# Seven products for eight in six weight pairs of eight, half of their weight sums added by a DMA, and two small regroupings

## The chip, the cores and the metric

The kernel runs on one core of one Trainium2 chip. The metric is the device time of one execution in microseconds (us); lower is better. Engines are named as the profile names them: PE (TensorE: matmuls, with their weight loads shown apart as PEld), DVE (VectorE), ACT (ScalarE), POOL (GpSimd) and SP (SyncE, which here only issues DMAs).

## The reference, cut to what matters

Two layers over 256 rows of width 2048, all in float32. Each layer is a mixer and an MLP, each between two RMS norms:

```python
for l in range(DEPTH):
    g = norm_g[l]
    u = rmsnorm(h, g[0])
    ...                                    # mixer: input projection, two head groups, output projection
    h = h + rmsnorm(y, g[1])
    u = rmsnorm(h, g[2])
    z = jnp.square(jax.nn.relu(u @ mlp_w1[l])) @ mlp_w2[l]
    h = h + rmsnorm(z, g[3])
```

`mlp_w1[l]` is 2048 x 8192, `mlp_w2[l]` is 8192 x 2048. The change lies in `u @ mlp_w1[l]`, which the kernel calls the first half of the MLP ("up"), and at the seam between the output projection and the MLP.

## The kernel before, in words

**Tiles.** The 256 rows are two tiles (t = 0, 1) of 128. A product runs with a 128x128 piece of the activations as stationary operand and a 128x512 piece of the weights as moving operand, into a PSUM bank of 128x512. To keep float32 accuracy every operand is split in two float32r parts, hi = the rounded value and lo = the rest, and a product takes three matmuls: x_hi·w_hi, x_hi·w_lo, x_lo·w_hi.

**Weights.** SP loads a weight tile `raw` of two 128-row slabs by 512 columns (512 KB). ACT casts it to `whi` (L223, or L331 in the MLP's first half), DVE subtracts to get `wlo` (L224, L332). There are 7 buffers for `raw` and 6 pairs for `whi`/`wlo`; a pair comes free when PE has done the last product that reads it, and a cast waits for a free pair.

**The MLP.** Its 8192 hidden columns are taken in 8 chunks of 1024. `up(c)` computes a chunk, `down(c)` multiplies it with `mlp_w2`. The order in the code is up(0), up(1), down(0), up(2), down(1), ..., up(7), down(6), down(7). Chunk 0 runs with ordinary blocks (`Block`), chunks 1 to 7 with `Pairs`; both layers do this, so there are 14 `Pairs` blocks in all.

**Pairs.** A `Pairs` block has eight steps s. Step s takes two slabs of 128 weight rows, 1024 columns wide, in two raw tiles: L (the first 512 columns) and R (the last 512), each with rows 0 and 1. This is a 2 x 2 block product: (t = 0, 1) x (row 0, 1) times (row 0, 1) x (L, R). The string `PAIRS`, one letter a step, says how it is computed:
- "C", ordinary: 8 products, that is 24 matmuls, into four banks p2, bR, q4, q3, with L and R cast as they are.
- "S", summed: the Strassen-Winograd form with 7 products (21 matmuls), called p1, p2, q3, q5, p7, p6, q4 in this order, each with a PSUM bank of its own over all steps. It needs sums of the activation blocks (made once a layer by `Differences`, L294 to L305) and of the weights: R1+R0 and R0+L0, from which `two` is cast, then L0+(R1+R0) and L1+(that), from which `four` is cast.

Before, `PAIRS` is "CSCSSCSS". `Pairs.load(s)` for an S step does, in the order of the code: the cast of L (`plain`), the cast of R's row 1 (`r1`), two DVE additions in place on R (L336), the cast of R (`two`), two DVE additions in place on L (L336), the cast of L (`four`). So an S step takes four pairs of `whi`/`wlo`, a C step two.

At the last step, which is an S, the block's results are combined from the seven banks on DVE (L383, L397, L398), with p1 and bR copied out by ACT (L387, L372), and `evac` applies the squared ReLU (L598).

**Order on the engines.** Each engine, and each DMA queue, works its instructions in a fixed order that is set when the program is built. The builder may place an instruction ahead of one that stands earlier in the code; what waits on what is kept by semaphores.

**The seam.** `out_proj` ends with four weight steps that run first for t = 0 and then for t = 1 (TAIL). `between(t)` follows each: it finishes the norm of the projection (L551, L552), adds to h (L509), transposes h for the next products (`prenorm_x`: PE L175, ACT L166, DVE L168), sums the squares of h on ACT (`sumsq_of`, L489) for the second norm, and stores h by POOL's DMA (L532). up(0) starts with six weight steps (LEAD) run for t = 0 alone, then `lead_in` calls `between(1)`, then the same six run for t = 1. The factor of the second norm is not needed before the last chunk of the MLP, since a squared ReLU lets it be applied late.

Of the kernel before, what the change touches and what calls it, by code (L numbers as in the profile page):

```python
# [22 lines left out]
NT = 2  # L23
# [4 lines left out]
PAIRS = "CSCSSCSS"  # L28
# [11 lines left out]
def trunk(ctx, tc, x, x_t, norm_g, ng_cols, e_win, rbf, e_wout, o_win, lbraw, smalls, wa2, ba, o_wout, w1, w2,  # L40
# [269 lines left out]
    class Pairs:  # L310
# [13 lines left out]
        def load(self, s):  # L324
            raws = [rawp.tile([P, SLAB, 512], F32, name="raw") for _ in range(2)]
            for raw, n in zip(raws, (self.n0, self.n0 + 512)):
                nc.sync.dma_start(out=raw, in_=self.wv[:, 2 * s:2 * s + 2, n:n + 512])

            def conv(raw, i=slice(0, SLAB)):
                hi, lo = w_pair()  # L330
                nc.scalar.copy(out=hi[:, i, :], in_=raw[:, i, :])  # L331
                nc.vector.tensor_tensor(out=lo[:, i, :], in0=raw[:, i, :], in1=hi[:, i, :], op=ALU.subtract)  # L332
                return hi, lo

            def add(dst, a, b):
                nc.vector.tensor_tensor(out=dst, in0=a, in1=b, op=ALU.add)  # L336
# [12 lines left out]
            self.w[s] = [plain, r1, two, conv(L)]  # L349

        def product(self, n, s, x, w, i):
            first = n not in self.ps
            if first:
                self.ps[n] = accp.tile([P, 512], F32, name="acc") if n in ("bR", "p2", "p1") else aux()
            ps, (xh, xl), (hi, lo) = self.ps[n], x, w
            done = s == self.nslab - 1 or n == "bR" and "C" not in PAIRS[s + 1:]
            nc.tensor.matmul(ps, xh, hi[:, i, :], start=first, stop=False)  # L357
            nc.tensor.matmul(ps, xh, lo[:, i, :], start=False, stop=False)  # L358
            nc.tensor.matmul(ps, xl, hi[:, i, :], start=False, stop=done and not (n == "bR" and i == 0))  # L359

        def mm(self, s, t):
# [4 lines left out]
            z = self.ps  # L366
            if PAIRS[s] == "C":
# [9 lines left out]
            s1, u, u3, zb = self.U  # L377
            out = {}

            def comb(n, a, b, op):  # L380
                if n not in out:
                    out[n] = self.evac.tile()
                nc.vector.tensor_tensor(out=out[n], in0=a, in1=b, op=op)  # L383

# [4 lines left out]
            if end:  # L389
                comb("aL", z["p2"], s1, ALU.add)  # L390
                self.evac(0, 0, out["aL"])
# [8 lines left out]
            if end:  # L400
                comb("aR", z["q5"], u, ALU.subtract)
                comb("aR", z["q3"], out["aR"], ALU.add)
                self.evac(0, 1, out["aR"])
                comb("bL", z["q4"], u3, ALU.add)
                self.evac(1, 0, out["bL"])
                comb("bR", z["q5"], u3, ALU.subtract)
                comb("bR", zb, out["bR"], ALU.add)
                self.evac(1, 1, out["bR"])
# [128 lines left out]
    def out_proj(l, w, kts, X2, y, X, ypool, spool, src, mid):  # L537
# [25 lines left out]
        return rst, lambda: between(1)  # L563

    def mlp(l, X, rst, y, ypool, spool, mid, between, lead):
# [11 lines left out]
        def lead_in():  # L577
            lead()
            for t in range(NT):
                pre[t] = powers(rst[t])  # L580
# [48 lines left out]
        def scratch():  # L629
            for _ in range(2):  # L630
                u = spool.tile([P, 2, 512], F32, name="s")
                U.extend(u[:, i, :] for i in range(2))
# [78 lines left out]
    def feed_forward(l, w, kts, X2, src, between):  # L711
        pools = [tc.tile_pool(name=f"yp{l}", bufs=1), tc.tile_pool(name=f"sp{l}", bufs=7)]
# [3 lines left out]
        rst, lead = out_proj(l, w, kts, X2, y, X, yp, sp, src, mid)  # L716
        mlp(l, X, rst, y, yp, sp, mid, lambda t, r, h: between(t, r, h, y, yp), lead)()
# [495 lines left out]
```

## Time and profile before

| | |
|---|---|
| time, median of 3 runs | 2261.35 us (2261.01 to 2261.88) |
| the profiled execution's own time | 2261.99 us |
| its span, first to last instruction | 2260.2 us |
| mean granted TensorE clock | 0.999 |
| PE busy | 2238.3 us, 99% of the span |
| DVE busy | 1750.7 us, 77% |
| ACT busy | 1173.7 us, 52% |
| DMA queue of SP (q1) | 429.18 MB, 59.1% of 16 engines' span |
| DMA queue of POOL (q0) | 8.99 MB, 1.1% |

A row of instructions reads: line of the kernel, engine, operation, output tile <- input tiles, shapes, count | busy us, mean ns of one | idle time of the engine before them and what ended it. A row of a timeline reads: start in us from the start of the span, duration in us, engine, line, operation. A matmul's duration is that of one matmul in a pipeline: the next one starts before it ends, so PE's pace is read from start to start.

### The profile page before, as it was taken

Reading aid. Unit: us, or ns where it says so; the run is one execution under the profiler, and the core shown is the slowest. Engines: PE = TensorE matmul, PEld = TensorE weight load, DVE = VectorE, ACT = ScalarE, POOL = GpSimd, SP = SyncE. Lnnn points to the kernel's source line nnn. Section 1 sums busy time; section 2 is a strip of 40 time slices with the busy share of each in tenths; the row PEclk is TensorE's granted clock in tenths of the full one; section 3 lists DMA queues with packets and bytes.
Section 4 is the critical chain, followed back from the end, with each engine's and each line's share of the span. In section 5 each row is a group of like instructions: output and inputs, shape, how many; then the busy total and the mean of one; then the engine's idle time right before and its main releaser. Section 6 shows DMA issues by size and latency. Waiting matters only on the chain.

```text
span 2260.2 us, 28830 instructions
## 1 busy us (share of the span) xinstructions
PE 2238.3 (99%) x10556; PEld 1850.9 (82%) x10556; DVE 1750.7 (77%) x2328; ACT 1173.7 (52%) x1612; POOL 20.7 (1%) x40
## 2 busy tenths in 40 slices
PE   9999999999999999999999999999999999999998
PEld 7888887888888888888788888887888888888886
DVE  6656656988898898896867767657979789789786
ACT  7444445655454454454746454546555445445453
POOL 0000000000000000000100000000000000000000
PEclk9999999999999999999999999999999999999999
DMA  9565576565665665676655555576565565665673
GB/s 344 168 182 168 168 268 186 181 222 165 198 216 160 211 198 184 205 242 221 213 172 166 153 151 153 173 237 194 169 205 195 187 206 184 197 205 177 214 263 102
DMA packets 222559, 440.87 MB, mean 195 GB/s; under 512 B 13744, under 2 KB 14544, under 8 KB 222416
## 3 DMA queue, kind: packets, MB, share of 16 engines
q1 hardware_dynamic: 218880, 429.18, 59.1%
q0 software_dynamic: 2816, 8.99, 1.1%
q8 instruction: 83, 1.36, 0.3%
q10 hardware_dynamic: 720, 0.85, 0.1%
q14 instruction: 60, 0.49, 0.1%
HBM read 430.57 MB, written 8.40 MB: 194 GB/s over the span
## 4 chain that ended last, share of the span: by engine, by line
PE 75%; DVE 14%; issue 5%; ACT 4%; DMA 1%; ACTq 0%; DVEq 0%; SPq 0%
PE acc L237 18%; PE acc L238 17%; PE acc L236 17%; DVE raw L336 4%; DVE wlo L332 4%; PE acc L275 3%; PE aux L275 3%; ACT whi L331 3%; DVE wlo L224 2%; PE aux L272 2%; PE acc L272 2%; DVE ulo L383 2%; PE aux L359 2%; PE aux L357 2%; PE aux L358 2%
## 5 line engine op out<-in xcount | busy, mean ns | idle before, releaser
L224 DVE TENSOR_TENSOR wlo<-raw,whi 128x1024 fp32r<-128x1024 f32 (+1 forms) x561 | 676.2, 1219 | 303.9 <-ACT whi L223 301.9
L223 ACT CAST whi<-raw 128x1024 fp32r<-128x1024 f32 (+1 forms) x561 | 582.5, 1053 | 587.1 <-PE acc L238 464.7
L331 ACT CAST whi<-raw 128x1024 fp32r<-128x1024 f32 x364 | 343.5, 969 | 372.3 <-DVE raw L336 213.8
L237 PE MATMUL acc<-wlo,x 128*128 128x512 f32 x1280 | 502.7, 393 | 1.9 <-DVE wlo L224 0.6
L238 PE MATMUL acc<-whi,x 128*128 128x512 f32 x1280 | 498.8, 390 | 0.0
L236 PE MATMUL acc<-whi,x 128*128 128x512 f32 x1280 | 497.1, 392 | 0.0
L332 DVE TENSOR_TENSOR wlo<-raw,whi 128x1024 fp32r<-128x1024 f32 x364 | 397.9, 1119 | 106.2 <-ACT whi L331 99.4
L237 PEld LDWEIGHTS acc<-wlo,x 128*128 128x128 f32 x1280 | 240.3, 188 | 59.2 <-DVE wlo L224 10.8
L236 PEld LDWEIGHTS acc<-whi,x 128*128 128x128 f32 x1280 | 240.3, 188 | 50.6
L238 PEld LDWEIGHTS acc<-whi,x 128*128 128x128 f32 x1280 | 240.4, 188 | 49.1
L236 PE MATMUL acc<-whi,xt 128*128 128x512 f32 x640 | 254.1, 399 | 0.5 <-ACT xt L671 0.5
L237 PE MATMUL acc<-wlo,xt 128*128 128x512 f32 x640 | 251.6, 394 | 3.0 <-DVE wlo L224 3.0
L238 PE MATMUL acc<-whi,xt 128*128 128x512 f32 x640 | 250.8, 392 | 0.0
L336 DVE TENSOR_TENSOR raw<-raw 128x512 f32<-128x512 f32 x280 | 193.8, 692 | 9.3
L237 PEld LDWEIGHTS acc<-wlo,xt 128*128 128x128 f32 x640 | 120.8, 189 | 29.6 <-DVE wlo L224 6.2
L236 PEld LDWEIGHTS acc<-whi,xt 128*128 128x128 f32 x640 | 120.6, 189 | 25.7 <-ACT xt L671 1.4
L238 PEld LDWEIGHTS acc<-whi,xt 128*128 128x128 f32 x640 | 120.5, 188 | 25.3 <-issue 0.3
L357 PE MATMUL acc<-whi,xt 128*128 128x512 f32 x308 | 120.0, 390 | 0.0
L359 PE MATMUL acc<-whi,xt 128*128 128x512 f32 x308 | 119.8, 389 | 0.0
L358 PE MATMUL acc<-wlo,xt 128*128 128x512 f32 x308 | 119.8, 389 | 0.0
L358 PE MATMUL aux<-wlo,s 128*128 128x512 f32 x280 | 110.6, 395 | 1.9 <-DVE wlo L332 0.2
L357 PE MATMUL aux<-whi,s 128*128 128x512 f32 x280 | 109.2, 390 | 0.0
(230 smaller groups left out, 2551.2 us busy)
## 6 DMA issues: line engine op xcount, KB each, us to landing
raw<-w SPq DMA_DIRECT2D x512, 512.0 KB, 4.5
raw<-o_win SPq DMA_DIRECT2D x112, 512.0 KB, 3.8
raw<-e_win SPq DMA_DIRECT2D x95, 512.0 KB, 3.9
raw<-e_wout SPq DMA_DIRECT2D x32, 512.0 KB, 4.2
raw<-o_wout SPq DMA_DIRECT2D x32, 512.0 KB, 3.7
s<-norm_g SPq DMA_DIRECT2D x8, 512.0 KB, 4.6
mid<-s POOLq DMA_DIRECT2D x8, 512.0 KB, 3.5
s<-mid SPq DMA_DIRECT2D x8, 512.0 KB, 5.7
```

Source lines behind the costliest of these rows:

```text
L223: nc.scalar.copy(out=hi[:, a:b, n], in_=raw[:, a:b, n])
L224: nc.vector.tensor_tensor(out=lo[:, a:b, n], in0=raw[:, a:b, n], in1=hi[:, a:b, n], op=ALU.subtract)
L236: nc.tensor.matmul(ps, xh, hi[:, i, 0:self.n], start=first, stop=False)
L237: nc.tensor.matmul(ps, xh, lo[:, i, 0:self.n], start=False, stop=False)
L238: nc.tensor.matmul(ps, xl, hi[:, i, 0:self.n], start=False, stop=last)
L275: nc.tensor.matmul(self.ps[j], hi[:, i, cs], x, start=s == 0 and i == 0, stop=False)
L331: nc.scalar.copy(out=hi[:, i, :], in_=raw[:, i, :])
L332: nc.vector.tensor_tensor(out=lo[:, i, :], in0=raw[:, i, :], in1=hi[:, i, :], op=ALU.subtract)
L336: nc.vector.tensor_tensor(out=dst, in0=a, in1=b, op=ALU.add)
L357: nc.tensor.matmul(ps, xh, hi[:, i, :], start=first, stop=False)
L358: nc.tensor.matmul(ps, xh, lo[:, i, :], start=False, stop=False)
L359: nc.tensor.matmul(ps, xl, hi[:, i, :], start=False, stop=done and not (n == "bR" and i == 0))
```

## The change

`PAIRS` becomes "SSSCSSSC": six S steps and two C steps in a block, C fourth and last. In an S step the two additions on R are taken from DVE: one DMA issued by POOL reads the same 1024 columns of weight row block 2s again from DRAM and adds them onto R in place (row 0 gets L0, row 1 gets R0). The combination of the seven banks is done at the last S step as far as it goes, and finished at the last C step from p2, q3, q4 and bR; the ACT copy of bR is gone. The sums of squares of h for the second norm leave `between` and stand at the loads of steps 6 and 8 of up(0). One more `Differences` a layer is made at the first step of up(1), and the pool of `s` tiles has 8 buffers for 7.

```diff
-PAIRS = "CSCSSCSS"
+PAIRS = "SSSCSSSC"
...
             plain = conv(L)
             r1 = conv(R, slice(1, 2))
-            add(R[:, 1, :], R[:, 1, :], R[:, 0, :])
-            add(R[:, 0, :], R[:, 0, :], L[:, 0, :])
+            nc.gpsimd.dma_start(out=R.rearrange("p a b -> p (a b)"), in_=self.wv[:, 2 * s, self.n0:self.n0 + 1024],
+                                accum_op=ALU.add)
             two = conv(R)
             add(L[:, 0, :], L[:, 0, :], R[:, 1, :])
             add(L[:, 1, :], L[:, 1, :], L[:, 0, :])
             self.w[s] = [plain, r1, two, conv(L)]
...
             if PAIRS[s] == "C":
-                for n, t, j in (("p2", 0, 0), ("bR", 1, 1), ("q4", 1, 0), ("q3", 0, 1)):
+                for n, t, j in (("p2", 0, 0), ("q3", 0, 1), ("q4", 1, 0), ("bR", 1, 1)):
                     for i in range(2):
                         self.product(n, s, x[t][i], w[j], i)
-                if "C" not in PAIRS[s + 1:]:
-                    nc.scalar.copy(out=self.U[3], in_=z.pop("bR"))
+                    if s == self.nslab - 1:
+                        o = self.out[t, j]
+                        if j == 0:
+                            add(o, z[n], s1 if t == 0 else u3)
+                        else:
+                            add(o, z[n], o)
+                        self.evac(t, j, o)
                 return
...
-            end = s == self.nslab - 1
+            end = "S" not in PAIRS[s + 1:]
...
             if end:
-                nc.vector.tensor_tensor(out=u, in0=z["p6"], in1=s1, op=ALU.add)
-                nc.vector.tensor_tensor(out=u3, in0=z["p7"], in1=u, op=ALU.add)
+                self.out = {(t, j): self.evac.tile() for t in range(NT) for j in range(2)}
+                add(u, z["p6"], s1)
+                add(u3, z["p7"], u)
+                add(self.out[0, 1], z["q5"], u, ALU.subtract)
+                add(self.out[1, 1], z["q5"], u3, ALU.subtract)
             self.product("q4", s, x[1][1], four, 1)
...
         def between(t):
             add_post(t, y, rsqrt_of(total(ss[t]), 1, 1.0 / D), h)
-            rst[t] = prenorm(t, h[t], l, 2, X, ypool)
+            prenorm_x(t, h[t], l, 2, X)
             for f in halves(h[t], lambda cs: mid[t, :, cs], nc.gpsimd):
                 f()
 
+        def factors(t):
+            rst[t] = prenorm_r(h[t], ypool)
...
         work = [lambda p=p: difference(p) for p in range(len(PAIRS)) if PAIRS[p] == "S"]
-        run(up(0), lead=lead_in, hooks={LEAD + 1 + 2 * i: [f] for i, f in enumerate(work)})
+        hooks = {LEAD + 1 + 2 * i: [f] for i, f in enumerate(work[:5])}
+        for t in range(NT):
+            hooks[LEAD + 2 * t] = [lambda t=t: norm(t)]
+        run(up(0), lead=lead, hooks=hooks)
         scratch()
         for c in range(1, NCH):
-            run(up(c))
+            run(up(c), hooks={0: work[5:]} if c == 1 else {})
```

`norm(t)` calls `factors(t)` and then the small `powers` of it, which `lead_in` did before.

More of the change, by code (lines that the diff above doesn't have):

```diff
@@ L355, in product @@
             ps, (xh, xl), (hi, lo) = self.ps[n], x, w
-            done = s == self.nslab - 1 or n == "bR" and "C" not in PAIRS[s + 1:]
+            if n in ("q5", "p7", "p6", "p1"):
+                stop = "S" not in PAIRS[s + 1:]
+            else:
+                stop = s == self.nslab - 1 and i == SLAB - 1
             nc.tensor.matmul(ps, xh, hi[:, i, :], start=first, stop=False)
             nc.tensor.matmul(ps, xh, lo[:, i, :], start=False, stop=False)
-            nc.tensor.matmul(ps, xl, hi[:, i, :], start=False, stop=done and not (n == "bR" and i == 0))
+            nc.tensor.matmul(ps, xl, hi[:, i, :], start=False, stop=stop)
         def mm(self, s, t):
@@ L366, in mm, with add @@
             z = self.ps
+            s1, u, u3 = self.U
+            def add(n, a, b, op=ALU.add):
+                nc.vector.tensor_tensor(out=n, in0=a, in1=b, op=op)
             if PAIRS[s] == "C":
-                for n, t, j in (("p2", 0, 0), ("bR", 1, 1), ("q4", 1, 0), ("q3", 0, 1)):
+                for n, t, j in (("p2", 0, 0), ("q3", 0, 1), ("q4", 1, 0), ("bR", 1, 1)):
                     for i in range(2):
                         self.product(n, s, x[t][i], w[j], i)
-                if "C" not in PAIRS[s + 1:]:
-                    nc.scalar.copy(out=self.U[3], in_=z.pop("bR"))
+                    if s == self.nslab - 1:
+                        o = self.out[t, j]
+                        if j == 0:
+                            add(o, z[n], s1 if t == 0 else u3)
+                        else:
+                            add(o, z[n], o)
+                        self.evac(t, j, o)
                 return
@@ L388, in mm @@
             self.product("p2", s, x[0][1], L, 1)
-            if end:
-                comb("aL", z["p2"], s1, ALU.add)
-                self.evac(0, 0, out["aL"])
             self.product("q3", s, d.get(3), r1, 1)
@@ L575, in finish, with norm @@
             between(t, rsqrt_of(sl[t], 1, None, base[t]), late["h"])
[L577 to L580, printed above, removed]
+        def norm(t):
+            factors(t)
+            pre[t] = powers(rst[t])
         def up(c):
```

27 lines of the change are left out of this document (6 added, 21 removed).

## The prediction

> **What bounds the kernel now.** I read the page's busy times and clock first, then the PE timeline of one `Pairs` block, to tell a busy PE from a PE at its pace.
>
> ```profile
> span 2260.2 us, 28830 instructions
> PE 2238.3 (99%) x10556; PEld 1850.9 (82%) x10556; DVE 1750.7 (77%) x2328; ACT 1173.7 (52%) x1612; POOL 20.7 (1%) x40
> PEclk9999999999999999999999999999999999999999
> ```
>
> PE is busy throughout at full granted clock: taking matmuls away should take time away, unless another engine falls behind. Two pieces of the timeline of up(2), in the second S step of a neighbouring two and in the block's last step:
>
> ```profile
> 543.78 0.39 PE L357 MATMUL aux<-whi,s 128*128 128x512 f32 x1
> 544.00 0.39 PE L358 MATMUL aux<-wlo,s 128*128 128x512 f32 x1
> 544.23 0.39 PE L359 MATMUL aux<-whi,s 128*128 128x512 f32 x1
> 544.46 0.39 PE L357 MATMUL aux<-whi,s 128*128 128x512 f32 x1
> ```
>
> ```profile
> 558.74 0.39 PE L357 MATMUL aux<-whi,s 128*128 128x512 f32 x1
> 559.25 0.50 PE L358 MATMUL aux<-wlo,s 128*128 128x512 f32 x1
> 559.59 0.40 PE L359 MATMUL aux<-whi,s 128*128 128x512 f32 x1
> 559.83 0.39 PE L357 MATMUL aux<-whi,s 128*128 128x512 f32 x1
> ```
>
> In the first piece three matmuls take 544.46 - 543.78 = 0.68 us, so a matmul costs 0.227 us, not its 0.39. In the second the same three take 1.09: PE loses 0.41 us waiting for the low part of `two`. Why, the rows by form and DVE's timeline show:
>
> ```profile
> L332 DVE TENSOR_TENSOR wlo<-raw,whi 128x1024 fp32r<-128x1024 f32 x294 | 354.5, 1222 | 93.4 <-ACT whi L331 86.6
> L332 DVE TENSOR_TENSOR wlo<-raw,whi 128x512 fp32r<-128x512 f32 x70 | 48.0, 686 | 12.8 <-ACT whi L331 12.8
> L336 DVE TENSOR_TENSOR raw<-raw 128x512 f32<-128x512 f32 x280 | 193.8, 692 | 9.3
> ```
>
> ```profile
> 557.98 2.50 DVE L332 TENSOR_TENSOR wlo<-raw,whi 128x1024 fp32r<-128x1024 f32 x2
> ```
>
> An S step costs DVE 3 x 1.222 + 0.686 + 4 x 0.692 = 7.12 us, a C step 2.44; PE needs 21 x 0.227 = 4.76 and 24 x 0.227 = 5.44. Over a block DVE has 5 x 7.12 + 3 x 2.44 = 42.9 us of weight work against PE's 177 x 0.227 = 40.1. DVE starts a block some buffers ahead and has used that up at the end: `two` and `four` of the last step are subtracted from 557.98 to 560.48, when PE needs them. So PE sets the time, and DVE touches it at each block's end.
>
> **Part 1, six S steps for five.** 3 matmuls less in each of 14 blocks: 42 x 0.227 = 9.5 us less on PE, all on the path. In trade DVE's block becomes 6 x (3 x 1.222 + 0.686 + 2 x 0.692) + 2 x 2.44 = 39.3 us, against PE's 174 x 0.227 = 39.4. By throughput DVE now just keeps up; and the block ends on a C step, so no `two` or `four` is fresh there. I take the 0.41 us of the block's end as gone: 14 x 0.41 = 5.7 us. What is next there is the combination (8 DVE operations before and after), now spread over the last two steps.
>
> **Part 2, the accumulating DMA.** It stands between the subtraction of `r1` and the cast of `two`; where it is late, `two` on ACT and all that stands behind it on ACT and DVE waits, and PE for that. The trace has no such DMA. Nearest is POOL's plain load of the same 512 KB:
>
> ```profile
> raw<-rbf POOLq DMA_DIRECT2D x2, 512.0 KB, 5.6
> ```
>
> ```profile
> DMA to landing us min/median/max: 4.2/5.6/7.0
> ```
>
> ```profile
> DMA packets 277, 0.81 MB, mean 135 GB/s; under 512 B 16, under 2 KB 16, under 8 KB 276
> ```
>
> ```profile
> DMA packets 1381, 3.48 MB, mean 386 GB/s; under 512 B 112, under 2 KB 112, under 8 KB 1381
> ```
>
> The last two rows are the DMA engines' traffic from 70 to 76 us, around the load of 4.2, and from 19 to 28 us, around that of 7.0. The accumulating DMA cannot be cheaper than a plain load, since it moves the same bytes and reads its target too: low end 4.2 us. High end: twice that, 8.4, if the second read costs as much as the whole. I take 5.6, the median: a block moves 166 GB/s and the `down` after it 219 (rows below), nearer to the quiet case, and the second read comes on top. The Trainium skill, "Collectives: The Full Stack", section "The bandwidth ceiling", says that a reducing copy runs at half the rate of a plain one since it reads two sources; no run here shows it. By that rule the sum would move toward my high end and the change would lose (second rival).
>
> How much time there is, the timeline tells (DVE, then ACT; the step whose q5 starts on PE at 543.78):
>
> ```profile
> 536.95 1.83 DVE L332 TENSOR_TENSOR wlo<-raw,whi 128x1024 fp32r<-128x1024 f32 x2 [0.32 <-ACT whi L331]
> 538.81 2.87 DVE L336 TENSOR_TENSOR raw<-raw 128x512 f32<-128x512 f32 x4
> 541.60 3.64 DVE L332 TENSOR_TENSOR wlo<-raw,whi 128x1024 fp32r<-128x1024 f32 x3
> ```
>
> ```profile
> 535.86 1.05 ACT L331 CAST whi<-raw 128x1024 fp32r<-128x1024 f32 x1 [0.49 <-PE aux L359]
> 537.22 0.62 ACT L331 CAST whi<-raw 128x512 fp32r<-128x512 f32 x1 [0.31 <-PE aux L359]
> 540.34 1.06 ACT L331 CAST whi<-raw 128x1024 fp32r<-128x1024 f32 x1 [2.50 <-DVE raw L336]
> ```
>
> The casts of `plain` and `r1` waited for PE to free a weight buffer (0.49 and 0.31 us). `r1` is done at 536.95 + 1.83 = 538.78; the second matmul of q5 starts at 544.00, and from the cast of `two` to the end of its subtraction go 541.60 + 1.22 - 540.34 = 2.48. That leaves 544.00 - 538.78 - 2.48 = 2.74 us for the sums, where two additions take 1.45 today and the DMA would take 5.6. In the code's order, then, it does not fit in the second and third S of a run of three. (The first S is converted during the `down` before it, where a buffer comes free with each weight step, 12 x 0.227 = 2.7 us, so it has several of those.)
>
> It fits if the next step's `plain` and `r1` are put ahead of this step's `two`. They then take the buffers that the running step frees after p1, p2 and q3, 9 x 0.227 = 2.04 us from its start T; cast and subtraction (0.62 + 0.69, and 0.15 for the hand-overs) end at T + 3.5. The sum is needed 2.48 us before the second matmul of q5 two steps on, T + 2 x 4.76 + 2.04 + 0.23 = T + 11.8, that is at T + 9.3: a window of 5.8 us. So 5.6 just fits. That the engines' orders leave the code's order where a wait would stand is in the trace: all four additions on L336 run before the subtraction of `two`, which the code has after the first two, and the casts of up(2) run between and ahead of the copies of down(0), which stands earlier in the code:
>
> ```profile
> 519.01 1.05 ACT L331 CAST whi<-raw 128x1024 fp32r<-128x1024 f32 x1 [2.29 <-DVE raw L336]
> 520.18 0.59 ACT L609 COPY y<-acc 128x512 f32<-128x512 f32 x1
> ```
>
> With a margin of 0.2 us some transfers will miss; I charge 0.1 us, half the margin, for each of 28 runs of three S steps: +2.8 us, an estimate. POOL has nothing queued behind these DMAs inside the MLP. On the DMA engines:
>
> ```profile
> 521.30:562.00 40.70, 40.57 (x179) 33.15 (x178) 35.30 (x40) 23.32 (x27) 0.00 (x0) 1.00 0.53 166
> 562.00:607.96 45.96, 45.80 (x209) 37.54 (x208) 38.30 (x46) 20.71 (x23) 0.00 (x0) 1.00 0.66 219
> ```
>
> Up and down move (40.70 x 166 + 45.96 x 219) / 1000 = 16.8 MB in 86.66 us at a mean share of 0.60. Six sums add 3.1 MB, or 6.3 with the second read: share 0.71 to 0.83. Loads land later but do not bound.
>
> **Part 3, the late sums of squares.** At the seam of layer 0 (ACT, then PE, then two rows of PE's waits):
>
> ```profile
> 387.92 0.75 ACT L489 ACTIVATE junk<-s 128x512 f32<-128x512 f32 x1
> 390.83 0.19 ACT L489 ACTIVATION_READ_ACCUMULATOR junk<-s 128x1 f32 x1
> 391.05 0.60 ACT L551 ACTIVATE junk<-acc 128x512 f32<-128x512 f32 x1
> ```
>
> ```profile
> 393.45 0.40 PE L238 MATMUL acc<-whi,xt 128*128 128x512 f32 x1
> 395.18 1.05 PE L175 MATMUL aux<-ident,s 128*128 128x128 f32 x6 [1.34 <-issue]
> ```
>
> ```profile
> PE aux L175 <- DVE s L509: 2.2, 3, 1.3
> PE aux L175 <- issue: 1.3, 1, 1.3
> ```
>
> ACT squares h of t = 0 for 3.1 us (387.92 to 391.02) and only then squares the projection of t = 1 (L551), from which the chain to the transposes goes. PE waits 1.3 us for these, once in each layer (the longest of the first wait, and the second). With the squares moved the chain is 3.1 us earlier, more than PE waits: 2.6 us gone. They then run beside up(0)'s casts, where ACT, at 52% of the span, has room; if not, at most the same 2.6 comes back.
>
> **Part 4, the sixth difference.** Beside up(1) DVE gets, once in each layer, one set of these:
>
> ```profile
> L301 DVE TENSOR_TENSOR relu<-relu 128x128 f32<-128x128 f32 x40 | 9.7, 283 | 0.1
> L294 DVE TENSOR_TENSOR relu<-xt 128x512 f32<-128x512 f32 x10 | 6.8, 683 | 0.1
> L305 DVE TENSOR_TENSOR s<-relu,s 128x512 fp32r<-128x512 f32 x10 | 6.8, 682 | 0.0
> ```
>
> That is 0.683 + 4 x 0.283 + 0.682 = 2.5 us, in a block in which DVE has 0.1 to spare: 0 to 5.0 us in two layers. It is needed only at step 6 and DVE waits for buffers early in a block; I take 1.0.
>
> **The sum.** -9.5 - 5.7 - 2.6 + 2.8 + 1.0 = -14.0 us. On the profiled 2261.99 us (span 2260.2 and 1.8 around it), which is 0.64 above the median, this gives 2248.0; on the median of 2261.35, 2247.4.
>
> **The rivals.** A measurement of this kernel can tell about 0.2% from no change, 4.5 us: 2256.8 to 2265.9 is "the same".
>
> First, the matmuls go and nothing else does: PE keeps 0.41 us at the block ends (the DMA's wait in place of the additions) and 28 small waits: -9.5 - 2.6 + 2.8 + 1.0 = -8.3, or 2253.
>
> Second, on the other side: the sum lands too late. Of what the landing exceeds 5.8 us, PE loses about that much once in each of the 28 runs (transfers of a run overlap). The gains without part 2's charge are 16.8 us, so it decides from 5.8 + 16.8 / 28 = 6.4 us on; at the crowded 7.0 it is 28 x 1.2 - 16.8 = +17, or 2278; at 8.4, 28 x 2.6 - 16.8 = +56, or 2317. For it: the second read, and that the sums go out while 53 to 66% of the DMA engines' time is taken. Against it: the median of 5.6 includes a crowded one. Between 6.2 and 6.6 us it is a draw, the third case.
>
> Fourth, the orders stay as the code has them. The second S of a run is then 5.6 - 2.74 = 2.9 us late. For the third, DVE goes from one landing to the next in 2.48 + 1.22 + 1.22 + 0.69 (`two`, `four`, `plain`, `r1`) + 5.6 = 11.2 us where PE needs 4.76: 6.4 lost. At least 9.3 a run: 28 x 9.3 - 16.8 = +244, or 2505. Against it stands the order that the trace shows.
>
> **How the numbers follow.** The forecast 0.47 and the first rival 0.10: faster 0.57. The draw: 0.11. Late sums 0.27 and the code's order 0.05: slower 0.32. The forecast's own range is 2243 (no charge for parts 2 and 4) to 2256. The range for 8 in 10 goes up to 2300, a landing of 7.8 us: it leaves out the code's order, some 0.10 of the late sums and 0.03 below 2243.
>
> **What would show it.** Right: 42 matmuls less on L357 to L359 (2436 for 2478) and L336 with 168 instead of 280; PE's three matmuls at 0.68 us in the third S step too and at the end of a block; the DMA's landing at or under 5.8 us; `plain` and `r1` of the next step ahead of `two` on ACT; no wait over 0.3 us at L175 after L238 at the two seams. Wrong: casts on L331 that wait for a DMA issued by POOL with PE waiting for `wlo` L332 behind them, above all in steps 1, 2, 5 and 6, or landings over 6.4 us; or blocks that end with PE waiting for the combination.

## The result and the profile after

| | before | after |
|---|---|---|
| time, median | 2261.26 us (2261.01 to 2261.88) | 2789.93 us (2787.84 to 2790.89) |
| ratio to before | | 1.2336, 95% interval 1.2316 to 1.2355 |
| span of the profiled execution | 2260.2 us | 2786.0 us |
| mean granted TensorE clock | 0.999 | 0.925 |

The change costs 529 us. The forecast was 2247.4, and the range ended at 2300. What came is the fourth rival (the engines keep the code's order), which had a chance of 0.05 and a price of 2505.

The page of the kernel after: its span, the engines' busy times, the clock, POOL's DMA queue, three groups of instructions (the idle time before them and what ended it stand last), and the DMA issues of `Pairs`.

```profile
span 2786.0 us, 29060 instructions
...
PE 2414.7 (87%) x10514; PEld 1930.8 (69%) x10514; DVE 1698.8 (61%) x2256; ACT 1188.0 (43%) x1628; POOL 92.1 (3%) x124
...
PEclk9999998989898898979999999998989989898989
...
q0 software_dynamic: 14912, 53.03, 10.4%
...
L331 ACT CAST whi<-raw 128x1024 fp32r<-128x1024 f32 x392 | 356.8, 954 | 744.4 <-DMA raw<-w 652.2
...
L336 DVE TENSOR_TENSOR raw<-raw 128x512 f32<-128x512 f32 x168 | 116.3, 692 | 596.5 <-DMA raw<-w 593.7
L360 PE MATMUL aux<-whi,s 128*128 128x512 f32 x336 | 174.7, 559 | 330.5 <-ACT whi L331 330.5
...
raw<-w POOLq DMA_DIRECT2D x84, 512.0 KB, 7.1
```

Read from the bottom: a sum lands 7.1 us after its issue; the casts on ACT and the additions on DVE stand idle for it (652 and 594 us, at the same time); PE stands idle for the casts (331 us); and where PE has stood idle, the clock falls. The waits say how often: 82 to 84 times, so for every one of the 84 sums.

```profile
ACT whi L331 <- DMA raw<-w: 652.2, 82, 11.5
DVE raw L336 <- DMA raw<-w: 593.7, 84, 10.1
...
PE aux L360 <- ACT whi L331: 330.5, 140, 8.3
```

One cycle of it, on ACT, then POOL, then DVE, in up(2) (the second S step's `two` is cast at 568.62, the third's at 581.60):

```profile
559.58 0.63 ACT L331 CAST whi<-raw 128x512 fp32r<-128x512 f32 x1
568.62 1.04 ACT L331 CAST whi<-raw 128x1024 fp32r<-128x1024 f32 x1 [8.41 <-DMA raw<-w]
570.13 2.52 ACT L331 CAST whi<-raw 128x1024 fp32r<-128x1024 f32 x3 [0.47 <-DVE raw L336]
581.60 1.04 ACT L331 CAST whi<-raw 128x1024 fp32r<-128x1024 f32 x1 [8.95 <-DMA raw<-w]
```

```profile
561.23 0.85 POOL L344 DMA_DIRECT2D raw<-w  x1 [10.80 <-DMA raw<-w]
574.48 0.85 POOL L344 DMA_DIRECT2D raw<-w  x1 [12.40 <-DVE wlo L332]
```

```profile
568.61 1.42 DVE L336 TENSOR_TENSOR raw<-raw 128x512 f32<-128x512 f32 x2 [7.68 <-DMA raw<-w]
569.94 4.24 DVE L332 TENSOR_TENSOR wlo<-raw,whi 128x1024 fp32r<-128x1024 f32 x4
581.59 1.42 DVE L336 TENSOR_TENSOR raw<-raw 128x512 f32<-128x512 f32 x2 [7.41 <-DMA raw<-w]
```

ACT casts `two`, `four`, `plain` and `r1` in the code's order and then stands still for the next `two`. The step from one landing to the next is 569.94 + 4.24 - 568.61 = 5.57 us of DVE, 574.48 - 574.18 = 0.30 to the issue and 581.59 - 574.48 = 7.11 to the landing: 12.98 us, for 4.76 us of PE's work.

Stretches of up(2), cut at PE's stalls (us, then busy time and count of PE, PEld, DVE, ACT and POOL; the last three numbers are the granted clock, the DMA engines' share and GB/s):

```profile
557.90:564.65 6.75, 6.47 (x29) 5.00 (x28) 2.96 (x3) 2.31 (x4) 0.85 (x1) 1.00 0.75 189
564.65:576.60 11.95, 7.64 (x22) 5.33 (x21) 5.48 (x6) 3.56 (x4) 0.85 (x1) 0.71 0.48 119
576.60:590.00 13.40, 8.07 (x23) 5.68 (x22) 7.76 (x8) 5.46 (x6) 0.27 (x1) 0.75 0.52 136
590.00:596.30 6.30, 6.30 (x29) 4.96 (x27) 0.00 (x0) 0.00 (x0) 0.58 (x1) 1.00 0.79 203
```

PE's clock is full while it runs through and 0.71 to 0.75 in the stretches with stalls. In the 3.4 us around the end of the first of them, 569.7, it is 0.50 (same columns):

```profile
568.60:572.00 3.40, 1.98 (x4) 1.17 (x5) 3.30 (x4) 2.91 (x3) 0.00 (x0) 0.50 0.00 0
```

The Trainium skill, "TensorE: Matmul & The Clock Gate", section "HAM oscillation — how this bites in real kernels", says that a wait for DMA can make the gate throttle again, so that the next tile starts at half rate; these windows agree, with 0.50 at the stall's end.

Counted from start to start of the block's matmuls, in all 14 blocks: what goes beyond 0.227 us a matmul is 536.5 us (before: 8.2), of which 383.5 in steps over 0.6 us (PE stands) and 150.6 in slower steps below that (PE runs at the low clock).

### The profile page after: what moved, and what is told of

Its sections match the earlier page's. It is cut to its first block, busy times and chain, and to the rows that moved or that the text cites. A ratio compares the mean times of both kernels' runs of the same rounds, so it can differ in the third digit from the quotient of the medians.

```text
span 2786.0 us, 29060 instructions
## 1 busy us (share of the span) xinstructions
PE 2414.7 (87%) x10514; PEld 1930.8 (69%) x10514; DVE 1698.8 (61%) x2256; ACT 1188.0 (43%) x1628; POOL 92.1 (3%) x124
## 3 DMA queue, kind: packets, MB, share of 16 engines
q0 software_dynamic: 14912, 53.03, 10.4%
## 4 chain that ended last, share of the span: by engine, by line
PE 42%; issue 27%; DMA 17%; DVE 10%; ACT 3%; POOL 0%; POOLq 0%; DVEq 0%; ACTq 0%; SPq 0%
DMA raw<-w 15%; PE acc L237 10%; PE acc L238 10%; PE acc L236 10%; PE acc L275 3%; PE aux L275 3%; DVE wlo L332 2%; DVE raw L336 2%; DVE wlo L224 2%; DVE ulo L373 1%; PE aux L272 1%; PE acc L272 1%; ACT whi L331 1%; PE aux L958 1%; ACT whi L223 1%
## 5 line engine op out<-in xcount | busy, mean ns | idle before, releaser
L331 ACT CAST whi<-raw 128x1024 fp32r<-128x1024 f32 x392 | 356.8, 954 | 744.4 <-DMA raw<-w 652.2
L336 DVE TENSOR_TENSOR raw<-raw 128x512 f32<-128x512 f32 x168 | 116.3, 692 | 596.5 <-DMA raw<-w 593.7
L360 PE MATMUL aux<-whi,s 128*128 128x512 f32 x336 | 174.7, 559 | 330.5 <-ACT whi L331 330.5
L332 DVE TENSOR_TENSOR wlo<-raw,whi 128x1024 fp32r<-128x1024 f32 x392 | 419.5, 1106 | 25.6 <-ACT whi L331 21.4
L360 PEld LDWEIGHTS aux<-whi,s 128*128 128x128 f32 x336 | 72.3, 237 | 409.1 <-ACT whi L331 403.7
L236 PEld LDWEIGHTS acc<-whi,x 128*128 128x128 f32 x1280 | 240.3, 188 | 52.6 <-ACT whi L223 3.2
L236 PE MATMUL acc<-whi,xt 128*128 128x512 f32 x640 | 253.8, 399 | 1.1 <-ACT xt L672 1.0
L237 PE MATMUL acc<-wlo,xt 128*128 128x512 f32 x640 | 250.9, 392 | 3.4 <-DVE wlo L224 2.1
L238 PE MATMUL acc<-whi,xt 128*128 128x512 f32 x640 | 250.5, 392 | 0.0
L361 PE MATMUL aux<-wlo,s 128*128 128x512 f32 x336 | 175.4, 522 | 0.0
L362 PE MATMUL aux<-whi,s 128*128 128x512 f32 x336 | 173.9, 518 | 0.0
L360 PE MATMUL acc<-whi,xt 128*128 128x512 f32 x280 | 115.4, 413 | 15.9 <-DVE y L609 12.9
```

What stands on the lines that cost most here:

```text
L236: nc.tensor.matmul(ps, xh, hi[:, i, 0:self.n], start=first, stop=False)
L237: nc.tensor.matmul(ps, xh, lo[:, i, 0:self.n], start=False, stop=False)
L238: nc.tensor.matmul(ps, xl, hi[:, i, 0:self.n], start=False, stop=last)
L362: nc.tensor.matmul(ps, xl, hi[:, i, :], start=False, stop=stop)
```

## The experiments

Three theories. A: the sum is started only after `r1` of its own step, in the code's order, and everything on ACT, DVE and PE waits out its landing. B: the added traffic makes loads late. C: three S steps in a row starve PE, whoever makes the sums.

**The additions back on DVE** (`adds_back`), all else as after:

```diff
-            nc.gpsimd.dma_start(out=R..., in_=self.wv[:, 2 * s, ...], accum_op=ALU.add)
+            add(R[:, 1, :], R[:, 1, :], R[:, 0, :])
+            add(R[:, 0, :], R[:, 0, :], L[:, 0, :])
```

> The changed kernel with the two additions on R back on DVE, no accumulating DMA. Theory A (time is lost because the cast of `two` waits for the sum's landing, about 7.1 us, while ACT and DVE keep the code's order): the 529 us go but for what DVE itself lacks, 47.6 us of weight work a block against PE's 39.4, some 2 to 6 us a block after the buffered lead: 2270 to 2340 us. Theory B (the 44 MB of extra traffic make the weight loads late): the same, 2270 to 2340. Theory C (three S steps in a row starve PE whoever makes the sums): still over 2600 us.

Measured 2339.86 us, ratio 1.0347 (1.0333 to 1.0361). So 450 of the 529 us go with the DMA, and the rest of the change (the order of steps, the sixth S step, parts 3 and 4) costs 78 by itself. One block and the `down` behind it, in the same columns:

```profile
713.40:757.20 43.80, 40.64 (x174) 32.05 (x173) 42.85 (x53) 26.06 (x29) 0.00 (x0) 1.00 0.51 164
757.20:804.40 47.20, 46.41 (x210) 37.93 (x209) 36.08 (x42) 18.77 (x21) 0.00 (x0) 1.00 0.64 204
```

DVE is busy for 42.85 of 43.80 us: a sixth S step with all its additions makes DVE the bound of the block, as the prediction's 7.12 us a step would have it (6 x 7.12 + 2 x 2.44 = 47.6).

**The DMA alone in the kernel before** (`dma_before`); order of steps and sums of squares as before:

```diff
-            add(R[:, 1, :], R[:, 1, :], R[:, 0, :])
-            add(R[:, 0, :], R[:, 0, :], L[:, 0, :])
+            nc.gpsimd.dma_start(out=R..., in_=self.wv[:, 2 * s, ...], accum_op=ALU.add)
```

> The kernel before, with nothing changed but the two additions onto R, which the accumulating DMA takes over in the code's order (five S steps, none in a row of three, no late sums). It splits the 529 us: the kernel with the adds put back had 78 for the new order of steps. If the wait for the landing alone does it (A): the four or five S steps a block that wait there lose 2 to 8 us each as in the kernel after, 2550 to 2710 us. If the DMA only hurts with three S steps in a row: under 2400 us.

Measured 2630.93 us, ratio 1.1633 (1.1617 to 1.1649). The same wait, 70 times for 70 sums:

```profile
ACT whi L331 <- DMA raw<-w: 487.4, 70, 11.1
DVE raw L336 <- DMA raw<-w: 420.0, 70, 9.6
```

The DMA alone costs 369 us and needs no run of three. With the 78 for the rest of the change that makes 447. Most of the last 82 is the number of sums, 84 for 70: one sum costs 369 / 70 = 5.3 us here and 450 / 84 = 5.4 in the kernel after, so 14 more make 74, and a run of three hardly makes a sum dearer.

**Traffic without a reader**, twice. First an accumulating DMA for each S step onto a `spare` tile in the kernel before (`traffic_only`):

```diff
             add(R[:, 0, :], R[:, 0, :], L[:, 0, :])
+            nc.gpsimd.dma_start(out=spare, in_=self.wv[:, 2 * s, ...], accum_op=ALU.add)
```

> The kernel before, all its additions on DVE, and in each of its 70 S steps the same accumulating DMA beside, onto a tile that nobody reads: the traffic without the wait. Theory A: no change, 2255 to 2270 us. Theory B: much of the loss shows, over 2400 us. Theory C: no change.

Measured 2364.58 us, ratio 1.0450 (1.0434 to 1.0466), but this did not test what it was meant to. The DMAs had nothing to wait for but each other, and POOL started all 70 one after another from the start of the program:

```profile
POOL spare L349 <- DMA spare<-w: 453.5, 69, 9.0
```

```profile
raw<-e_win SPq DMA_DIRECT2D x95, 512.0 KB, 7.0
```

The first mixer's weight loads then landed in 7.0 us instead of 3.9, and much of the time was lost there. Another 36 us of the 103 went in the first `Pairs` block (77 us for 41.6; all others kept their length), for another reason: the store of h (`mid`) stood on POOL's queue behind the 70 DMAs, ACT's part of the differences waited for it, and PE for ACT:

```profile
ACT s L307 <- DMA mid<-s: 34.7, 1, 34.7
...
PE acc L361 <- ACT relu L590: 32.6, 1, 32.6
```

So the DMA was tied to its place, by a one-column copy on POOL (`traffic_in_place`):

```diff
+            nc.gpsimd.tensor_copy(out=spare[:, 0:1], in_=r1[1][:, 1, 0:1])
+            nc.gpsimd.dma_start(out=spare, in_=self.wv[:, 2 * s, ...], accum_op=ALU.add)
             add(R[:, 1, :], R[:, 1, :], R[:, 0, :])
```

> The kernel before, all sums by VectorE, and beside them one accumulating DMA of 512 KB for each S step onto a tile that nobody reads, started in its place: a one-column copy on GpSimd from r1's lower half, into the first column of that tile, holds it until r1 is done, as in the kernel after. The traffic is that of the kernel after without anybody waiting for it (70 DMAs against 84). Theory A: 2261 us, 2255 to 2275. Theory B: over 2400 us, in proportion to the DMAs.

Measured 2265.15 us, ratio 1.0016 (1.0006 to 1.0026). The sums' traffic, issued where the change issues it, costs 4 us when nobody waits for it (70 sums for 84). B falls for traffic at this pace.

**The landing shorter** (`plain_load`), in the kernel after. The kernel leaves out the adding: R then holds the weights that were loaded and not the sum.

```diff
-            nc.gpsimd.dma_start(out=R..., in_=self.wv[:, 2 * s, ...], accum_op=ALU.add)
+            nc.gpsimd.dma_start(out=R..., in_=self.wv[:, 2 * s, ...])
```

> The kernel after, whose DMA onto R is a plain load of the same 512 KB by the same queue, so that R holds the first half's weights alone and not the sum: the output is not the reference's. The wait is the same, the landing shorter by what the accumulation costs. With 7.1 us for the accumulating DMA and 4.2 to 5.6 for plain ones, five S steps a block in 14 blocks wait 1.5 to 2.9 us less: 2590 to 2690 us. If accumulation costs nothing at the landing and the queue's own start does: 2760 to 2800 us.

Measured 2601.22 us, ratio 1.1502 (1.1481 to 1.1523). POOL's queue and landing:

```profile
q0 software_dynamic: 14912, 53.03, 6.2%
...
raw<-w POOLq DMA_DIRECT2D x84, 512.0 KB, 4.5
```

2.6 us less for each landing (7.1 to 4.5) take 189 us away, 2.25 us for each of 84 sums: the landing lies on the path nearly one for one. What accumulation costs the DMA engines is in the shares: 10.4% of 16 x 2786.0 us is 4636 us with it, 6.2% of 16 x 2596.7 is 2576 without; the queue's other transfers took 1.1% of 16 x 2260.2 = 398 in the kernel before, so the sums take 4238 / 2178 = 1.95 times the time of plain loads. The landing grows less, by a factor of 1.6. The Trainium skill, "Collectives: The Full Stack", section "The bandwidth ceiling", has a reducing copy at half the rate of a plain one because of its two source reads; the 1.95 agrees.

**PE kept busy in the wait** (`warm_fill`): the kernel after with matmuls of zeros behind q3.

```diff
             self.product("q3", s, d.get(3), r1, 1)
+            for _ in range((0, 8, 22, 0, 9, 20, 21)[s]):
+                nc.tensor.matmul(self.ps["q3"], zeros[:, 0:P], zeros, start=False, stop=False)
```

> The kernel after with matmuls of zeros (bf16, 512 columns) put into TensorE's order behind the product q3, where it waits for the sum: 8, 22, 9, 20 and 21 of them in the S steps with 2, 5, 2, 4.4 to 7.9 and 5 to 7.3 us of idle time. They add nothing to the result. The time of the waits is set by the landing and stays. If the slower matmuls behind each wait (a granted clock of 0.71 to 0.79 in those windows, some 150 us of TensorE time over the 14 blocks) lie on the path that sets the end: the clock rises to 1.0 and the time falls to about 2640 us (2600 to 2700). If the chain of conversions and landings sets the end alone and slow matmuls are hidden in it: 2790 us, within 30. If the zeros themselves stand in the way: over 2790.

Measured 2765.31 us, ratio 1.2231 (1.2212 to 1.2249): 25 us less, not 150. The block up(2) after and with the zeros:

```profile
558.10:635.20 77.10, 53.10 (x174) 38.82 (x173) 37.54 (x43) 27.54 (x32) 4.25 (x5) 0.80 0.56 143
```

```profile
558.10:632.70 74.60, 63.76 (x254) 42.24 (x253) 37.41 (x40) 27.27 (x32) 4.26 (x5) 0.93 0.55 146
```

The clock rose from 0.80 to 0.93 and the block became 2.5 us shorter. The zeros hardly stood in the way: behind 60 of the 70 groups the next product started 0.05 us after the cast that it waited for. Over the 14 blocks the slow steps fell from 150.6 to 76.0 us and the long ones rose from 383.5 to 440.0. The landings set the time, and most of the slow matmuls lie under them: the low clock is mainly a consequence, with a price of its own of about 25 us for the half that was removed.

**The late sums alone** (`late_only`): the kernel before with part 3 of the change.

> The kernel before with the late sums of squares alone. As predicted: PE's wait of 1.3 us at each of the two seams goes, 2258.8 us. Rival (the wait is handed on to the next thing that ACT does late): 2261.3 us.

Measured 2259.48 us, ratio 0.9991 (0.9982 to 1.0000): 2.1 us less than before's 2261.57, within what a measurement can tell from no change. PE's wait for the seam's additions to h, 2.2 us in 3 waits before, is 1.0 in 2, and PE's 1.3 us for "issue" is gone:

```profile
PE aux L175 <- DVE s L509: 1.0, 2, 0.5
```

**The order that the prediction assumed** (`pipelined`): loads, `plain`, `r1` and the DMA of step s+1 stand in the code ahead of `two` and `four` of step s.

```diff
         def load(self, s):
-            ...
+            if s == 0:
+                self.head(0)               # loads, plain, r1, DMA
+            if s + 1 < self.nslab:
+                self.head(s + 1)
+            self.rest(s)                   # two, additions on L, four
```

> The changed kernel with the order turned in the code: the loads, `plain`, `r1` and the DMA of step s+1 stand ahead of `two` and `four` of step s. Theory A: the sum has a window of 5.8 us where it takes 7.1; 28 runs lose about 1.3 us each on top of 2244.4: about 2281 us, 2245 to 2330. Theories B and C: the order does not matter, over 2600 us.

Measured 2443.22 us, ratio 1.0804 (1.0789 to 1.0819). 347 of the 529 us come back, and it still misses A's range. POOL in one block:

```profile
740.87 0.86 POOL L345 DMA_DIRECT2D raw<-w  x1 [8.50 <-DVE wlo L334]
754.50 0.85 POOL L345 DMA_DIRECT2D raw<-w  x1 [12.78 <-DVE wlo L334]
756.24 0.85 POOL L345 DMA_DIRECT2D raw<-w  x1 [0.89 <-DMA raw<-w]
768.55 0.85 POOL L345 DMA_DIRECT2D raw<-w  x1 [11.45 <-DVE wlo L334]
```

The first two sums behind the C step are issued 1.74 us after each other; they land 7.6 and 8.3 us after their issue, where the one at 740.87 takes 5.5. Three of the four rows wait for `wlo` of `r1`, and on ACT and DVE that still stands behind an earlier sum. ACT, from the landing of the sum of 754.50 on:

```profile
762.21 1.04 ACT L333 CAST whi<-raw 128x1024 fp32r<-128x1024 f32 x1 [7.68 <-DMA raw<-w]
763.73 2.52 ACT L333 CAST whi<-raw 128x1024 fp32r<-128x1024 f32 x3 [0.47 <-DVE raw L354]
```

These are `two`, then `four`, `plain` and `r1`; the sum that needs this `r1` goes out at 768.55, 6.4 us behind the landing. A weight buffer is not what holds them inside the block: over the run ACT's casts on L333 wait 172.5 us for landings and 37.0 for the block's own products to free a pair (131.0 more for those of the `down` ahead of it).

**The sum free of `r1`.** `r1` gets a small tile of its own, so that the DMA has only R's load to wait for. Once in the kernel before with the late sums (`own_r1_five`), once in the kernel after (`own_r1`, six raw buffers for room):

```diff
+            R1 = rawp.tile([P, 512], F32, name="r1", bufs=2)
+            nc.sync.dma_start(out=R1, in_=self.wv[:, 2 * s + 1, self.n0 + 512:self.n0 + 1024])
+            nc.gpsimd.dma_start(out=R..., in_=self.wv[:, 2 * s, ...], accum_op=ALU.add)
             plain = conv(L)
-            r1 = conv(R, slice(1, 2))
-            ...                            # the additions on R, or the DMA
+            r1 = w_pair()                  # cast and difference from R1
```

> The kernel before (its order of steps, C S C S S C S S, and its adds of the last half) with the late sums, and the sums of R by the accumulating DMA with r1 from its own tile, started as soon as R has landed; seven raw buffers. Theory A: the DMA is hidden, VectorE has two additions of 0.69 us a step less, TensorE has the same matmuls as before: 2250 to 2270 us, the same as the kernel with the late sums alone or slightly better. Theory B: over 2350 us. Theory C: about 2255 us, since no three S steps follow each other; with own_r1 over 2340 that would be C.

> The kernel after, but r1 is made from a small tile of its own (256 KB more loaded by SyncE for each S step), so that the accumulating DMA has only R's own load to wait for and not r1's two conversions; six raw buffers instead of seven. The same bytes are summed by the same DMA. Theory A (what cost 529 us is that the sum is started only after r1 of its own step, on engines that keep the code's order): the sum starts as soon as R has landed, some two steps ahead of its use, and its landing of about 7 us is covered; 2245 to 2300 us, and the wait of ScalarE for the sum falls from 652 us to under 100. Theory B (the accumulating traffic itself makes loads late): over 2400 us, with the waits moved to the plain loads. Theory C (three S steps in a row starve TensorE whoever makes the sums): not under the 2340 of the kernel with the adds put back.

`own_r1_five`: 2251.46 us, ratio 0.9965 (0.9954 to 0.9976), faster than before and the fastest kernel of this case; it stands 8 us below the late sums alone. `own_r1`: 2329.54, ratio 1.0304 (1.0288 to 1.0319), outside A's range. With five S steps the DMA pays, at the same 7.0 us of landing; its sums are awaited 33 us in all, and a block runs at PE's pace (177 matmuls in 39.90 us):

```profile
raw<-w POOLq DMA_DIRECT2D x70, 512.0 KB, 7.0
```

```profile
ACT whi L331 <- DMA raw<-w: 33.2, 15, 3.7
```

```profile
604.00:643.90 39.90, 39.90 (x177) 33.03 (x176) 30.31 (x33) 23.34 (x26) 2.56 (x3) 1.00 0.84 239
643.90:690.40 46.50, 45.95 (x210) 37.71 (x209) 37.19 (x45) 20.61 (x23) 1.71 (x2) 1.00 0.79 241
```

So A is the cause of the 369 us: the same sums with the same landing cost nothing once `r1` does not stand in front of them. With six S steps the DMA does not pay, though by my sum DVE has only 39.3 us of weight work in a block. That was the open question: the order, the raw buffers, or the sixth S step.

**What six S steps cost.** Six kernels, all with the sum free of `r1`: `own_r1_piped` (order after, the turned code of `pipelined`), `own_r1_six` (PAIRS "SSCSSCSS" in before's code), `five_raw6` (five, one raw buffer less), `six_raw7` and `after_raw7` (seven raw buffers kept, r1's tile put in the slots of the scratch tile `relu`), `piped_raw7` (the turned code with that).

```diff
-PAIRS = "CSCSSCSS"
+PAIRS = "SSCSSCSS"                         # own_r1_six, six_raw7
...
-RAW_BUFS = 7
+RAW_BUFS = 6                               # own_r1, own_r1_piped, own_r1_six, five_raw6
...
-            R1 = rawp.tile([P, 512], F32, name="r1", bufs=2)
+            R1 = ypool.tile([P, 512], F32, name="relu", bufs=2)    # six_raw7, after_raw7, piped_raw7
```

> The kernel with r1 from its own tile (2329.5 us), and the code's order turned: the loads, plain and r1 of step s+1, and its DMA, stand ahead of two and four of step s. In the kernel with the own r1, ScalarE stood still for some 2 to 2.7 us in most S steps between its cast of two and that of four, while VectorE made the difference of two and the two additions (an S step took 6.9 to 7.7 us there, TensorE's part of it 4.76); with plain and r1 of the next step in that gap, an S step takes VectorE's 5.7 us or less. If this handing over in the code's order is what three S steps in a row still cost (A, the same cause as with the landing): 2245 to 2280 us. If VectorE's and ScalarE's sheer work, or the six weight buffers, set it (C): 2310 to 2340 us, no better than without the turn.

> The kernel with r1 from its own tile in before's order of steps and late sums (five S steps, 2251.5 us), with a sixth S step in place of the first C: S S C S S C S S, six raw buffers instead of seven for room, and the sixth set of differences made in the second block. 42 matmuls of 0.227 us less, minus 9.5, and one set of differences more, about 1 us each layer. If runs of two S steps stay covered, as in the kernel with five: 2241 to 2250 us. If the first pair, with no C step behind the half before it, or the sixth raw buffer's loss starves TensorE: 2255 to 2300 us.

> The kernel with r1 from its own tile and five S steps (2251.5 us), with six raw buffers instead of seven and nothing else. In the kernels with six S steps and six buffers the sum of the last S step was issued late, since R's slot came free late. If the missing raw buffer is what 65 to 78 us went to there: 2265 to 2310 us. If it is the sixth S step itself (its conversions, its 1.25 MB more of sums and loads a block): 2250 to 2258 us.

> The kernel S S C S S C S S with r1 from its own tile (2317.0 us), with r1's tile in the slots of another scratch tile that is idle then, and the room given to a seventh raw buffer. If the buffers are the cause: 2241 to 2262 us, the six S steps pay at last. If the sixth S step's own work or traffic is: 2300 to 2320 us.

> The same with the order of steps of the kernel after, S S S C S S S C, with r1 from its own tile and seven raw buffers (2329.5 us with six). If the buffers are the cause: 2245 to 2270 us. If three S steps in a row are, whatever the buffers: 2305 to 2330 us, and six_raw7 stands below it.

> The kernel with r1 from its own tile, the order S S S C S S S C and seven raw buffers (2330.9 us), with plain, r1 and the DMA of step s+1 ahead of two and four of step s in the code. If the handing over between ScalarE and VectorE is what three S steps in a row cost, the turn takes it out: 2270 to 2300 us, of which some 24 are the first block of each layer, whose r1 tiles wait for the differences. If the raw buffers, held longer by the turn, set the time instead: 2330 us or more, with the waits behind the second C step, where three sums are started together.

| order of steps | six raw buffers | seven |
|---|---|---|
| five S, C S C S S C S S | `five_raw6` 2276.82 (1.0071; 1.0056 to 1.0086) | `own_r1_five` 2251.46 |
| six S in pairs, S S C S S C S S | `own_r1_six` 2317.01 (1.0246; 1.0232 to 1.0260) | `six_raw7` 2283.70 (1.0096; 1.0079 to 1.0113) |
| six S, S S S C S S S C | `own_r1` 2329.54 | `after_raw7` 2330.86 (1.0304; 1.0289 to 1.0319) |
| the same, turned | `own_r1_piped` 2350.76 (1.0392; 1.0378 to 1.0407) | `piped_raw7` 2348.83 (1.0386; 1.0356 to 1.0417) |

`own_r1_six`, `six_raw7` and `own_r1_piped` lie outside all that was expected of them, `after_raw7` by 1 us.

So: one raw buffer less costs 25 us with five, 33 with six in pairs, and nothing with three in a row. The sixth S step costs 32 us with the buffers kept, of which some 23 are the first block of each layer (53.1 and 52.6 us, for 41.3 in the kernel before). There `relu` is also the scratch of the differences, and r1's load waits for it, which is this experiment's doing; PE's waits for `r1`'s cast are some 4.5 us of each of these two blocks, and the rest of their loss is not taken apart. Four of the later blocks of the second layer take 39.3 us, PE's pace for 174 matmuls. Three in a row cost another 47. Blocks of `six_raw7` and of `after_raw7`:

```profile
1797.20:1836.50 39.30, 39.30 (x175) 32.48 (x174) 32.95 (x37) 24.23 (x28) 2.54 (x3) 1.00 0.90 257
```

```profile
709.20:751.80 42.60, 40.48 (x174) 32.05 (x173) 35.37 (x42) 26.05 (x29) 2.56 (x3) 1.00 0.81 241
```

In the second, DVE is busy for 35.4 of 42.6 us and ACT for 26.1: neither is full, and the block is 3.3 us longer than the other. ACT's timeline shows why:

```profile
726.34 1.05 ACT L331 CAST whi<-raw 128x1024 fp32r<-128x1024 f32 x1 [3.14 <-DMA raw<-w]
730.08 2.00 ACT L331 CAST whi<-raw 128x1024 fp32r<-128x1024 f32 x2 [2.70 <-DVE raw L336]
731.98 0.61 ACT L348 CAST whi<-relu 128x512 fp32r<-128x512 f32 x1
732.94 1.06 ACT L331 CAST whi<-raw 128x1024 fp32r<-128x1024 f32 x1 [0.34 <-DMA raw<-w]
736.58 2.00 ACT L331 CAST whi<-raw 128x1024 fp32r<-128x1024 f32 x2 [2.58 <-DVE raw L336]
```

Between the cast of `two` and that of `four` ACT waits 2.6 to 2.7 us for DVE, which first makes the difference of `two` and adds. From `two` to `two` is 732.94 - 726.34 = 6.60 us, against PE's 4.76. My reading is that a C step gives that back, and that three S steps in a row lose it faster than the six weight buffers can hold. Turning the code takes most of these gaps away, but in `piped_raw7` PE loses 3.8 to 5.0 us in one place instead, in 12 of the 14 blocks, at the first sum behind the C step, and the time is 18 us worse. By the code the turn holds each raw tile a step longer; yet a seventh raw buffer wins only 2 us in this order, so that the raw buffers are the cause is not shown. The wait in one of its blocks:

```profile
PE aux L376 <- DVE wlo L334: 3.9, 1, 3.9
```

That the one wait goes and the other comes with the turn is shown; that they are all of the 47 us is not. An order with both cured was not found. So of theory C some 78 us stand (2329.54 for 2251.46), for a sixth S step and for three in a row, with a cause that is in part open.

## Why the prediction was wrong

**The failed step** is in part 2: "It fits if the next step's `plain` and `r1` are put ahead of this step's `two`", and the evidence for it, that "the engines' orders leave the code's order where a wait would stand". They did not: ACT and POOL kept the code's order in the kernel after, with 9 us of idle time in front of `two`. The two reorderings that I had quoted were real (the additions on L run ahead of the difference of `two` after the change as well, at 568.61), but they move an instruction past a neighbour of its own step or past an evacuation; nothing in the trace moved a weight conversion past another step's. Why the builder moves the one and not the other, no trace shows. The step that followed failed too: that in the assumed order `r1` ends at T + 3.5 and leaves a window of 5.8 us. In `pipelined`, which has that order, a sum's issue still follows an earlier landing, by 6.4 us in the rows shown, and 182 of the 529 us remain. The working had all that was needed: 2.74 us of room for a transfer of 4.2 or more "does not fit", at any landing between the bounds. It should have carried the forecast, not 0.05.

**The price of the fourth rival** was too low, 244 where 529 came. Its cycle was right in form (2.48 + 1.22 + 1.22 + 0.69 = 5.61 us of conversions; measured 5.57) and short in the landing (5.6; measured 0.30 + 7.11): 12.98, not 11.2. It gave the first S step of a run no loss; the trace has no wait for its landing at the block's start, but 1.0 to 3.9 us, from block to block, at the first S behind the C step. PE's idle time is 27.4 us a block, for 18.6 in the sum. And it had no term for the clock: 10.8 us a block of slow steps, most of which the landings would have filled anyway. The account of the profiled executions (2786.0 for 2260.2 us, +525.8): 536.5 - 8.2 = +528.3 in the blocks' steps, -9.5 for the matmuls, and the rest, +7, outside the blocks, the late sums' -2 among it; no run takes that rest apart.

**The landing.** I took 5.6 between 4.2 and 8.4; it was 7.1 median, on the side of the rival that I had thought less likely. Even with 4.5 (`plain_load`) the change loses 15%, so this mis-sized term did not decide. In the assumed order the median landing was 5.7, inside my window of 5.8, and the kernel still stood at 2443: the size was near, and what `r1` waits for was wrong.

**Part 1.** 42 matmuls less are there (PE x10514 for x10556). "By throughput DVE now just keeps up" left out a bound: the ACT-DVE alternation inside an S step takes 6.6 us in `after_raw7`, where DVE's work is 5.7. The 0.41 us at a block's end do go when DVE has fewer additions, but with five S steps: from a block's first matmul to its last go 39.9 us in `own_r1_five`, for 40.3 in the kernel before.

**Part 3** fits: -2.1 measured for -2.6, with the waits at the seam gone as forecast; the time alone, whose interval ends at 1.0000, hardly tells it from no change. **Part 4** was not measured alone. **DMA traffic** was right: 4 us in place (`traffic_in_place`).

**The second rival** had the right place, the sum's landing, but charged only what exceeds a window of 5.8 us, once a run; in the code's order a step pays its landing whole. So its worst case of 2317 and the range's 2300 fell short.

## What to carry to other kernels

Before a transfer replaces an engine's instruction, write down the in-order queue that issues it, the instruction that releases it and the one that waits for it; if the room between them is shorter than the nearest landing in the trace, the room is the forecast, unless a quoted row shows that very kind of instruction moved. A transfer that adds to a tile paid here once nothing of its own step released it: with the sums started at R's load five S steps were 0.35% faster (late sums included), with the same landing that cost 369 us behind `r1`. Two engines that hand a tile to and fro within a step can set that step's time although neither is full, as in the 6.6 us of `after_raw7`. And count the transfers before calling a cost an interaction: 14 more sums at 5.3 us each were most of the 82 us.

## What the runs showed of the hardware

- An accumulating DMA of 512 KB takes 1.95 times the DMA engines' time of a plain one in the same place, and lands in 7.1 us instead of 4.5.
- PE stalls of 2 to 8 us brought the granted clock to 0.71 to 0.79 in the stretches around them, and to 0.50 in 3.4 us around the end of one; keeping PE busy with zeros raised it from 0.80 to 0.93 in a block, for 25 us of 529.
- POOL issued 70 DMAs that waited only for each other one after another from the start of the program: the landing of SP's loads in the first mixer rose from 3.9 to 7.0 us, and a store behind them on POOL's queue came so late that PE stood for 32.6 us.
- Two sums issued 1.74 us apart landed in 7.6 and 8.3 us, one by itself in 5.5 (`pipelined`).
